# The first tiles of a two-layer hybrid-attention kernel: norm gain by VectorE shuffle, more idle products, another order of the first loads, and mixing products over 128 rows

## The chip, the cores and the metric

The kernel runs on one NeuronCore of a Trainium2 chip, in one launch. The metric is the time of an execution on the device in microseconds (us); of the kernel before there are three runs, and their median counts. Engines are named as the profile names them: PE is TensorE's products, PEld its weight loads, DVE is VectorE, ACT is ScalarE, POOL is GpSimd, SP is the queue engine that issues most DMAs.

## What is computed

Two layers over 512 tokens of 1024 features, then a last normalisation. Cut to what matters here:

```python
def rmsnorm(x, g):
    y = x * lax.rsqrt(jnp.mean(x * x, axis=-1, keepdims=True) + RMS_EPS)
    return y * g

def hybrid_layer(x, norm_g, w_in, ...):
    h = rmsnorm(x, norm_g)
    proj = h @ w_in                      # 1024 x 8388: queries, keys, values, gates
    ya = moba_attention(...);  yb = dsa_attention(...);  yc = dilated_mixture(...)
    merged = sum of sigmoid gates times (ya, yb, yc) @ w_br
    return x + merged @ w_out

def dilated_mixture(q, k, v):            # three groups with windows of their own
    ...
    w = softmax(stack(lses), axis=0)     # one weight a token, head and group
    return sum(w[..., None] * stack(outs), axis=0)
```

## The kernel before

A plan is built first: `add` records each operation with its engine, an estimate of its time, its buffers and a priority (`pri`, lower goes first), and `schedule` places them in order of start and priority on a modelled clock. What is emitted is that order; each engine runs its row of instructions in order and waits at semaphores. Priorities around -1e5 to -9e5 are those of the start.

All large products are taken in three parts, since a 32-bit number is split into a rounded upper part (`whi`, `h_hi`: a cast, L331, mostly on ACT) and the remainder (`wlo`, `h_lo`: a subtraction, L337 on POOL or L338 and L390 on DVE): hi by hi, hi by lo, lo by hi. So one tile of weights costs a DMA (`ws`), a cast, a subtraction and three products of 512 columns (L449 to L451 where the tokens are stationary, L430 to L432 where the weights are).

**The start.** x comes in four tiles t of 128 tokens, each in two halves b of 512 features (`load_x`, L286 to L296): one DMA of 256 KB for each. All go to SP's queue but the second half of tile 0, which goes to ACT's. `XPRI` sets how the later tiles stand among the first weight loads. For each tile: squares of both halves summed into `sq` (L668 ACT, L669 DVE), then `rstd`: mean plus epsilon (L738), root (L739, ACT), reciprocal (L740) and one Newton step (L741, L742, which leaves a factor -2). `norm_tile` multiplies x by that and by the gain, L711, into `h`; four transposes on PE (L717) put `h` into PSUM, a cast and a subtraction make `h_hi` and `h_lo` in the layout that the products want.

The gain `norm_g` of layer 0 is spread to 128 partitions by `first_g`: 4 KB come into one partition (`grow`, L304, third on ACT's queue), and two products of one row (L700) with a row of -0.5 (`half`) write it to PSUM as `gp`. The -0.5 undoes the factor -2. In layer 1 and for the last normalisation a DMA spreads the gain and ACT multiplies it by -0.5 (L685).

PE has idle products on zeros (`idle`, L325, `WARM` = 10 of them; `keep_warm`, L692, four after the gain and four behind each half of the transposes of tile 0) ahead of the first real one.

The first real products are `values` of the dilated groups (`c_values`): 512 columns of `w_in`, eight tiles of weights k, four tiles of tokens t. `VRUNS` lists the runs (t, first k, last k): tiles 0 and 1 take k 0 to 2 each, then 3 to 4, then 5 to 7; after that tiles 2 and 3 take all eight.

**The mixing** (`c_mix`, L1084 to L1094, once a layer): the softmax weights of the three groups are transposed into `rw`, whose other rows POOL clears first; for each pair of heads and each group one product with the constant `sel` (L1094) spreads twelve rows of `rw` over 128 partitions of `bc`, which multiplies the group's output (L1064, DVE). `rw` and `sel` are used in their rows 0 to 63. These products stand between other ones on PE in runs of 2, 1, 2 and 1.

## Time and profile before

| | |
|---|---|
| median of three runs | 1074.54 us (1073.83 to 1074.83) |
| the profiled execution, its own time | 1073.64 us |
| span of its instructions | 1071.9 us |
| PE busy | 1062.5 us (99%), 5390 products |
| PEld busy | 885.9 us (83%) |
| POOL busy | 637.5 us (59%) |
| ACT busy | 592.0 us (55%) |
| DVE busy | 510.9 us (48%) |

The execution's own time is 1.7 us longer than the span, and 0.9 us shorter than the median. Products overlap in the pipeline, so a product's duration is longer than the distance from one start to the next; distances between starts are what to read. Idle products count as busy like any others. The clock row of the page stands at full speed from the first slice on, though the first idle products are twice as far apart as the later ones; the level in the first microseconds is read from those distances.

### The profile page before, as it was taken

To read this page: it belongs to the slowest core of one execution; us is meant where nothing else is said; L and a number is where in the kernel's file an instruction comes from. 1 tells how busy PE (TensorE), PEld (TensorE's weight loads), DVE (VectorE), ACT (ScalarE), POOL (GpSimd) and SP (SyncE) were. 2 spreads that over 40 slices of the span, in tenths; PEclk is the share of its full clock that TensorE was granted. 3 is DMA by queue.
4 is the path that set the end of the run, shared out by engine and by line. 5 is a ranking of instruction groups with operands and counts; after the bars stand their busy time and mean duration, and the time that the engine had idled before them with its cause. 6 is when DMAs were issued, how large, how long until landed. Compare 5 with 4: busy or idle time off the path is not lost.

```text
span 1071.9 us, 16877 instructions
## 1 busy us (share of the span) xinstructions
PE 1062.5 (99%) x5390; PEld 885.9 (83%) x5390; DVE 510.9 (48%) x1434; ACT 592.0 (55%) x1493; POOL 637.5 (59%) x636
## 2 busy tenths in 40 slices
PE   9999999999999999999999999999999999999997
PEld 5898888888887878888888889888888878788885
DVE  5138987566642441113432589856655425311143
ACT  6444356787776653334553444568877767333441
POOL 4765754557753349776666177545666425686853
PEclk9999999999999999999999999999999999999999
DMA  7653543433431323453754155334444223336322
GB/s 227 186 125 79 148 109 83 140 83 94 120 94 51 81 60 99 110 175 98 217 160 130 30 136 145 85 95 112 112 101 119 65 52 81 87 89 194 109 81 78
DMA packets 123690, 119.00 MB, mean 111 GB/s; under 512 B 19385, under 2 KB 102225, under 8 KB 123602
## 3 DMA queue, kind: packets, MB, share of 16 engines
q1 hardware_dynamic: 123312, 117.61, 40.3%
q8 instruction: 42, 0.69, 0.3%
q14 instruction: 46, 0.38, 0.1%
q10 hardware_dynamic: 290, 0.33, 0.1%
HBM read 96.07 MB, written 6.36 MB: 96 GB/s over the span
## 4 chain that ended last, share of the span: by engine, by line
PE 98%; ACT 1%; issue 1%; DVE 0%; POOL 0%; POOLq 0%
PE pp L430 22%; PE pp L432 21%; PE pp L431 21%; PE sc L542 4%; PE pp L451 3%; PE pp L450 3%; PE pp L449 3%; PE po L1150 3%; PE po L1149 3%; PE po L1151 3%; PE tp L614 2%; PE pv L637 2%; PE pv L649 1%; PE sc L999 1%; PE pv L1037 1%; PE tpn L717 1%
## 5 line engine op out<-in xcount | busy, mean ns | idle before, releaser
L337 POOL TENSOR_TENSOR wlo<-ws,whi 128x256 fp32r<-128x256 f32 (+2 forms) x439 | 439.4, 1016 | 314.7 <-ACT whi L331 260.9
L430 PE MATMUL pp<-h_hi,whi 128*128 128x512 f32 (+1 forms) x896 | 357.1, 399 | 0.4 <-DVE gate L526 0.3
L432 PE MATMUL pp<-h_hi,wlo 128*128 128x512 f32 (+1 forms) x896 | 348.4, 389 | 0.0
L431 PE MATMUL pp<-h_lo,whi 128*128 128x512 f32 (+1 forms) x896 | 348.2, 389 | 0.0
L331 ACT CAST whi<-ws 128x256 fp32r<-128x256 f32 (+2 forms) x434 | 214.7, 508 | 236.1 <-PE pp L431 123.8
L432 PEld LDWEIGHTS pp<-h_hi,wlo 128*128 128x128 f32 x896 | 168.2, 188 | 35.1
L430 PEld LDWEIGHTS pp<-h_hi,whi 128*128 128x128 f32 x896 | 168.5, 188 | 34.3 <-issue 3.5
L431 PEld LDWEIGHTS pp<-h_lo,whi 128*128 128x128 f32 x896 | 168.6, 188 | 28.7
L873 DVE SCALAR_TENSOR_TENSOR th<-th,pp 128x512 f32<-128x512 f32 x32 | 22.0, 687 | 132.0 <-PE pp L432 126.8
L390 DVE TENSOR_TENSOR ptl<-tp,pth 128x256 fp32r<-128x256 f32 (+3 forms) x128 | 58.1, 462 | 44.0 <-ACT pth L331 43.3
L449 PE MATMUL pp<-whi,h_hi 128*128 128x512 f32 (+2 forms) x192 | 67.5, 352 | 0.0
L451 PE MATMUL pp<-whi,h_lo 128*128 128x512 f32 (+2 forms) x192 | 66.8, 348 | 0.0
L450 PE MATMUL pp<-wlo,h_hi 128*128 128x512 f32 (+2 forms) x192 | 66.7, 347 | 0.0
L331 ACT CAST pth<-tp 128x256 fp32r<-128x256 f32 (+3 forms) x128 | 50.7, 406 | 26.1 <-PE tp L614 15.0
L858 ACT ACTIVATE th<-pp 128x512 f32<-128x512 f32 x48 | 28.6, 595 | 54.6 <-PE pp L432 54.6
L552 ACT ACTIVATE p<-p,st 128x128 f32<-128x128 f32 (+3 forms) x96 | 53.5, 558 | 1.8 <-DVE st L550 1.5
L609 ACT ACTIVATE p<-p,st 128x128 f32<-128x128 f32 (+3 forms) x96 | 50.9, 558 | 1.8 <-DVE st L608 1.4
L820 DVE MATCH_REPLACE8 work<-m,work 128x512 f32<-128x512 f32 (+2 forms) x96 | 51.8, 542 | 0.1
L819 DVE MAX8 m<-work 128x8 f32<-128x512 f32 (+2 forms) x96 | 50.8, 550 | 0.7 <-POOL work L812 0.4
L430 PE MATMUL pp<-yh,whi 128*128 128x512 f32 x128 | 50.7, 396 | 0.0
L1149 PE MATMUL po<-whi,mhh 128*128 128x512 f32 x128 | 50.2, 392 | 0.0
L432 PE MATMUL pp<-yh,wlo 128*128 128x512 f32 x128 | 50.0, 391 | 0.0
(189 smaller groups left out, 1732.3 us busy)
## 6 DMA issues: line engine op xcount, KB each, us to landing
ws<-in_w_in_dram SPq DMA_DIRECT2D x192, 256.0 KB, 2.9
ws<-in_w_in_dram SPq DMA_DIRECT2D x96, 128.0 KB, 2.3
ws<-in_w_out_dram SPq DMA_DIRECT2D x32, 256.0 KB, 2.6
ws<-in_w_in_dram SPq DMA_DIRECT2D x24, 192.0 KB, 2.9
x<-x SPq DMA_DIRECT2D x16, 256.0 KB, 3.9
x<-in_x_dram SPq DMA_DIRECT2D x15, 256.0 KB, 5.1
zq<-rt SPq DMA_DIRECT2D x48, 64.0 KB, 2.8
zq<-rt SPq DMA_DIRECT2D x20, 128.0 KB, 2.4
```

The costliest lines, as they stand in the source:

```text
L331: add("act", n_act(n), lambda: nc.scalar.copy(dst(), src()), r=r, w=w, pri=pri, name=name, alt=("dve", n_dve(n, two), lambda: nc.vector.te ...
L337: add("pool", n_pool(n), lambda: nc.gpsimd.tensor_tensor(dst(), a(), b(), op), r=r, w=w, pri=pri, name=name, alt=("dve", n_dve(n), lambda: ...
L390: add("dve", n_dve(n), lambda: nc.vector.tensor_tensor(lo_fn(), src_fn(), hi_fn().bitcast(F32), ALU.subtract), r=[src, hi] if hi is not lo ...
L430: nc.tensor.matmul(o, lhs(hi.t, k % 2), a, start=(k == 0), stop=False)
L431: nc.tensor.matmul(o, lhs(hi.t, k % 2), b, start=False, stop=False)
L432: nc.tensor.matmul(o, lhs(lo.t, k % 2), a, start=False, stop=(k == nk - 1))
L449: nc.tensor.matmul(ps.t[:, :width], tokfn(h_hi, k), hi.t[:, kk, :width], start=(k == 0), stop=False)
L450: nc.tensor.matmul(ps.t[:, :width], tokfn(h_hi, k), lo.t[:, kk, :width], start=False, stop=False)
L451: nc.tensor.matmul(ps.t[:, :width], tokfn(h_lo, k), hi.t[:, kk, :width], start=False, stop=(k == KD - 1))
L552: add("act", n_act(N, True) + 190, lambda: nc.scalar.activation(p.t[:, :N], p.t[:, :N], AF.Exp, bias=nm_fn(), scale=-1.0, accum_out=s_fn() ...
L820: add("dve", n_dve(N) + 80, lambda i=i, N=N: nc.vector.match_replace(works[i].t[:, :N], m8[i].t, works[i].t[:, :N], GONE), r=[works[i], m8 ...
L1149: nc.tensor.matmul(ps.t[:, :n], mh.t[:, c], hi.t[:, kk, :n], start=(k == 0), stop=False)
```

## The change

- `first_g`, its two one-row products, `half` and the four idle products behind them go. `grow` becomes two tiles of 128x512, cleared by DVE; each half of `norm_g` comes by one small DMA into partitions 0, 32, 64 and 96 (ACT's queue, behind `ident`), and a VectorE shuffle (`spread_g`) copies the first row of each group of 32 partitions to all 32. The shuffle of the second half stands behind the first half's L711.
- Both halves of tile 0 of x go to SP's queue, first and second; `XPRI` places the other tiles anew. The preload of the root's table waits until the gain's DMAs are issued, and the first casts of the weights (`go`) wait for the first root.
- 18 idle products at the start; three and two behind the transposes of tile 0 (before: four and four).
- The constants of the root take over the factor: the mean is scaled by -4/D and the root taken with scale -1. The ACT multiplication by -0.5 becomes a plain copy in layer 1 and goes for the last normalisation.
- `VRUNS`: tiles 0 and 1 take k 0 to 4, then 5 to 7. `EARLY` goes to 0, so the first remainder is not given to DVE.
- The mixing products use all 128 rows of `rw` and `sel`; POOL clears 128 rows.

```diff
-WARM = 10
-VRUNS = ((0, 0, 3), (1, 0, 3), (0, 3, 5), (1, 3, 5), (0, 5, 8), (1, 5, 8), (2, 0, 8), (3, 0, 8))
-EARLY = 0.6
-XPRI = (0, 0.3, 1.6, 4.3)
+WARM = 18
+VRUNS = ((0, 0, 5), (1, 0, 5), (0, 5, 8), (1, 5, 8), (2, 0, 8), (3, 0, 8))
+EARLY = 0.0
+XPRI = (0, 0.6, 2.8, 4.4)
...
-        if l == 0 and t == 0 and b == 1 and not after:
-            add("act", 60, fn(nc.scalar), w=[xb], pri=-9e5, lag=2600.0)
-        else:
-            add("sp", 950 if l == 0 else 700, fn(nc.sync), r=[x1tok[t][b]] if l else (), w=[xb],
-                pri=-1e5 + XPRI[t] if t else -3e5, lag=2000.0, after=after)
+        add("sp", 950 if l == 0 else 700, fn(nc.sync), r=[x1tok[t][b]] if l else (), w=[xb],
+            pri=-1e5 + XPRI[t] if t else -3e5, lag=2000.0, after=after)
...
-            add("act", 60, lambda: nc.scalar.dma_start(grow.t[0:1, :], norm_g[0:1, :]), w=[grow], pri=-8e5, lag=3000.0)
-            add("act", 60, lambda: nc.scalar.dma_start(ident.t, k_ident), w=[ident], pri=-7e5, lag=3200.0)
+
+            add("act", 60, lambda: nc.scalar.dma_start(ident.t, k_ident), w=[ident], pri=-9e5, lag=3600.0)
+            for b in range(2):
+                add("dve", 550, lambda b=b: nc.vector.memset(grow[b].t, 0.0), w=[grow[b]], pri=-9e5)
+                loaded = add("act", 60, lambda b=b: nc.scalar.dma_start(grow[b].t[0:P:32, :], norm_g[0:1, b * T:(b + 1) * T].to_broadcast([4, T])),
+                    r=[grow[b]], w=[grow[b]], pri=-8e5, lag=2600.0)
...
-            copy(tot, lambda hi=hi: f(hi), lambda s=s: f(s), [s], [hi], pri, "whi", True)
+            copy(tot, lambda hi=hi: f(hi), lambda s=s: f(s), [s, go], [hi], pri, "whi", True)
...
-    def first_g():
...
-            add("pe", 870, lambda b=b: nc.tensor.matmul(g[b].t, half.t[0:1, 0:P], grow.t[0:1, b * T:(b + 1) * T], start=True, stop=True),
-                r=[half, grow], w=[g[b]], pri=-4e5, name="gb")
-        keep_warm(4, plan.ops[-1:])
-        return g
+    def spread_g(b, g, after):
+
+        add("dve", n_dve(T), lambda: nc.vector.stream_shuffle(g.t, grow[b].t, [0] * 32), r=[grow[b]], w=[g],
+            pri=-2e5 - 1, after=after, name="gb")
...
+            if not port and t == 0:
+                spread_g(b, gb[b], [hn] if b else ())
...
-                keep_warm(4, plan.ops[-1:])
+                keep_warm(3 - b, plan.ops[-1:])
...
-        tiny(lambda: stt(r.t[:, 1:2], c(6), -3.0, r.t[:, 0:1], op0=ALU.add, op1=ALU.mult), [st.tok], r)
+        tiny(lambda: stt(r.t[:, 1:2], c(6), 3.0, r.t[:, 0:1], op0=ALU.add, op1=ALU.mult), [st.tok], r)
...
-    preload((), -4e5)
+    preload([loaded], -4e5)
...
-            add("pool", n_pool(T) / 2, lambda: nc.gpsimd.memset(rw.t[0:64].bitcast(F32), 0.0), w=[rw], pri=pri, after=plan.ops[-1:])
+            add("pool", n_pool(T) / 2, lambda: nc.gpsimd.memset(rw.t.bitcast(F32), 0.0), w=[rw], pri=pri, after=plan.ops[-1:])
...
-                        nc.tensor.matmul(bc.t, sel.t[0:64, 2 * g + pr, :], rw.t[0:64], start=True, stop=True)
+                        nc.tensor.matmul(bc.t, sel.t[:, 2 * g + pr, :], rw.t, start=True, stop=True)
```

How the emitted rows move, engine by engine. DVE, from the first sum of squares on, before; `x_112` is the first half of tile 0 and `sq_93` holds the sums, `gp` is the spread gain and `wlo_169` the remainder of the first weight tile:

```order
L669 ISA sq_93 128x1
L738 ISA sq_93<-sq_93,invd 128x4
L738 ISA sq_93 128x1
L740 RECIPROCAL rstd_148<-sq_93 128x1
L741 SCALAR_TENSOR_TENSOR sq_93<-sq_93,rstd_148 128x1
L742 SCALAR_TENSOR_TENSOR rstd_148<-sq_93,rstd_148 128x1
L711 SCALAR_TENSOR_TENSOR h_164<-x_112,rstd_148,gp_134 128x512
L738 ISA sq_93<-sq_93,invd 128x4
L738 ISA sq_93 128x1
L338 TENSOR_TENSOR wlo_169<-ws_127,whi_162 128x512
```

and DVE after; `x_107` is the first half of tile 0, and the two `grow` tiles are the halves of the gain:

```order
L700 STREAM_SHUFFLE gp_126<-grow_91 128x512
L670 ISA junk_133,sq_109<-x_107 128x512
L670 ISA sq_109 128x1
L738 ISA sq_109<-sq_109,invd 128x4
L738 ISA sq_109 128x1
L740 RECIPROCAL rstd_154<-sq_109 128x1
L741 SCALAR_TENSOR_TENSOR sq_109<-sq_109,rstd_154 128x1
L742 SCALAR_TENSOR_TENSOR rstd_154<-sq_109,rstd_154 128x1
L711 SCALAR_TENSOR_TENSOR h_162<-x_107,rstd_154,gp_126 128x512
L700 STREAM_SHUFFLE gp_168<-grow_101 128x512
```

The two shuffles stand ahead of the square and ahead of the second half's L711, and the remainder `wlo` has left DVE.

ACT from its first row, before; `x_91` is the second half of tile 0, `x_118` the first half of tile 1:

```order
L305 DMA ident<-in_ident_dram 128x128
L293 DMA x_91<-in_x_dram 128x512
L304 DMA grow_95<-in_norm_g_dram 1x1024
L727 ACT_TABLE_LOAD
L727 ACTIVATE pre_107<-invd 128x1
L668 ACTIVATE junk_131,sq_93<-x_91 128x512
L668 ACTIVATE junk_139,sq_93<-x_118 128x512
L739 ACTIVATE sq_93<-sq_93 128x1
```

and after, where `x_118` is the second half of tile 0, `x_129` the first half of tile 1, `ws_122` the first weight tile:

```order
L302 DMA ident<-in_ident_dram 128x128
L305 DMA grow_91<-in_norm_g_dram 4x512
L305 DMA grow_101<-in_norm_g_dram 4x512
L727 ACT_TABLE_LOAD
L727 ACTIVATE pre_115<-invd 128x1
L669 ACTIVATE junk_140,sq_109<-x_118 128x512
L739 ACTIVATE sq_109<-sq_109 128x1
L332 CAST whi_150<-ws_122 128x512
L669 ACTIVATE junk_158,sq_109<-x_129 128x512
```

The root L739 of tile 0 has moved ahead of the squares of tile 1, x has left ACT's queue, and the gain takes two DMAs.

SP from its first row, before: `x_112` is tile 0, `x_118` and `x_122` tile 1, `x_158` and `x_167` tile 2:

```order
L293 DMA x_112<-in_x_dram 128x512
L293 DMA x_118<-in_x_dram 128x512
L293 DMA x_122<-in_x_dram 128x512
L284 DMA ws_127<-in_w_in_dram 128x512
L284 DMA ws_136<-in_w_in_dram 128x512
L284 DMA ws_144<-in_w_in_dram 128x512
L293 DMA x_158<-in_x_dram 128x512
L293 DMA x_167<-in_x_dram 128x512
L284 DMA ws_186<-in_w_in_dram 128x512
```

and after: `x_107` and `x_118` are tile 0, `x_129` and `x_137` tile 1, `x_175` is tile 2:

```order
L293 DMA x_107<-in_x_dram 128x512
L293 DMA x_118<-in_x_dram 128x512
L284 DMA ws_122<-in_w_in_dram 128x512
L293 DMA x_129<-in_x_dram 128x512
L293 DMA x_137<-in_x_dram 128x512
L284 DMA ws_146<-in_w_in_dram 128x512
L284 DMA ws_152<-in_w_in_dram 128x512
L284 DMA ws_164<-in_w_in_dram 128x512
L293 DMA x_175<-in_x_dram 128x512
L284 DMA ws_190<-in_w_in_dram 128x512
```

Tile 0 is whole ahead of the first weights, and tile 2 has moved behind the fourth weight tile. From the end of the products of tiles 0 and 1 on, PE's rows are the same before and after, but for the names' numbers.

## Rows read from the trace of the kernel before

**Rows 1.** Page, part 1: busy us, share of the span and instructions of each engine.
```profile
PE 1062.5 (99%) x5390; PEld 885.9 (83%) x5390; DVE 510.9 (48%) x1434; ACT 592.0 (55%) x1493; POOL 637.5 (59%) x636
```

**Rows 2.** Waits of PE, whole span: engine, line, releaser: us in total, times, longest.
```profile
PE sc L542 <- DVE mixt L550: 0.4, 2, 0.2
```

**Rows 3.** Timeline of PE from 0 to 16 us: start, us, operation [idle before].
```profile
1.00 4.45 PE L325 MATMUL warm<-idle 128*128 128x512 bf16 x10 [1.00 <-POOL idle L322]
5.38 3.78 PE L700 MATMUL gp<-grow,half 1*128 1x512 f32 x4
9.09 1.89 PE L692 MATMUL warm<-idle 128*128 128x512 bf16 x4
10.77 1.09 PE L717 MATMUL tpn<-ident,h 128*128 128x128 f32 x4
11.66 1.91 PE L692 MATMUL warm<-idle 128*128 128x512 bf16 x4
...
13.95 1.03 PE L692 MATMUL warm<-idle 128*128 128x512 bf16 x4
14.69 0.52 PE L449 MATMUL pp<-whi,h_hi 128*128 128x512 f32 x1
```

**Rows 4.** Timeline, DVE and ACT, 4 to 10.7 us.
```profile
4.01 0.69 DVE L669 CUSTOM_DVE_ANT_0 junk<-x 128x512 f32<-128x512 f32 x1 [3.09 <-DMA x<-in_x_dram]
...
6.54 0.63 ACT L668 ACTIVATE junk<-x 128x512 f32<-128x512 f32 x1 [2.79 <-DMA x<-in_x_dram]
...
7.37 0.17 DVE L738 CUSTOM_DVE_ANT_0 sq<-sq,invd 128x4 f32<-128x4 f32 x1 [2.60 <-ACT junk L668]
...
8.30 0.16 ACT L739 ACTIVATE sq<-sq 128x1 f32<-128x1 f32 x1
...
9.21 0.17 DVE L740 RECIPROCAL rstd<-sq 128x1 f32<-128x1 f32 x1 [1.66 <-ACT junk L668]
...
9.94 0.75 DVE L711 SCALAR_TENSOR_TENSOR h<-x,rstd,gp 128x512 f32<-128x512 f32 x1
```

**Rows 5.** Timeline, ACT and DVE, the same chain near the end.
```profile
1050.20 0.16 ACT L739 ACTIVATE sq<-sq 128x1 f32<-128x1 f32 x1 [5.17 <-DVE sq L738]
...
1050.38 0.17 DVE L740 RECIPROCAL rstd<-sq 128x1 f32<-128x1 f32 x1 [0.28 <-ACT sq L739]
```

**Rows 6.** Timeline, DMA issues on SP and ACT, and landing times of all x transfers until 30 us.
```profile
0.75 1.33 SPq L293 DMA_DIRECT2D x<-in_x_dram  x3
...
1.67 0.54 ACTq L304 DMA_DIRECT2D grow<-in_norm_g_dram  x1
...
DMA to landing us min/median/max: 4.2/4.7/5.1
```

**Rows 7.** Timeline of POOL, first long run of weight remainders.
```profile
17.35 5.06 POOL L337 TENSOR_TENSOR wlo<-ws,whi 128x512 fp32r<-128x512 f32 x4 [3.00 <-ACT whi L331]
```

**Rows 8.** Timeline of PE, mixing products of layer 0.
```profile
392.60 0.39 PE L431 MATMUL pp<-h_lo,whi 128*128 128x512 f32 x1
392.83 0.40 PE L432 MATMUL pp<-h_hi,wlo 128*128 128x512 f32 x1
393.16 0.73 PE L1094 MATMUL bc<-rw,sel 64*128 64x512 f32 x2
...
394.15 0.40 PE L431 MATMUL pp<-h_lo,whi 128*128 128x512 f32 x1
...
395.08 0.39 PE L432 MATMUL pp<-h_hi,wlo 128*128 128x512 f32 x1
395.40 0.50 PE L1094 MATMUL bc<-rw,sel 64*128 64x512 f32 x1
...
396.16 0.39 PE L431 MATMUL pp<-h_lo,whi 128*128 128x512 f32 x1
```

**Rows 9.** Timeline of PE's weight loads there, and all products of bc by tile.
```profile
393.16 0.29 PEld L1094 LDWEIGHTS bc<-rw,sel 64*128 64x128 f32 x2 [0.36 <-issue]
...
L1094 PE MATMUL bc<-rw,sel x12: 387/497/502, 393.2 to 925.1; 64*128 64x512 f32 x12
```

More of the change, by code (lines that the diff above doesn't have):

```diff
@@ L286, in hybrid_kernel @@
     fills = []
-    grow, half = buf("pt", [P, D], F32, "grow"), buf("rt", [P, T], F32, "half")
+    grow = [buf("rt", [P, T], F32, "grow") for _ in range(2)]
     def load_x(l, t, b, after):
@@ L316, in hybrid_kernel @@
     add("pool", 100, lambda: nc.gpsimd.memset(scol.t[64:128], 1.0), w=[scol])
-    add("pool", 100, lambda: nc.gpsimd.memset(invd.t, 1.0 / D), w=[invd])
+    add("pool", 100, lambda: nc.gpsimd.memset(invd.t, -4.0 / D), w=[invd])
     add("pool", 100, lambda: nc.gpsimd.memset(big.t, BIG), w=[big])
@@ L323, in hybrid_kernel @@
     warm = buf("pp", [P, T], F32, "warm")
-    for _ in range(WARM):
-        add("pe", 427, lambda: nc.tensor.matmul(warm.t, idle.t, idle.t[:, 0:1].to_broadcast([P, T]), start=True, stop=True), r=[idle], w=[warm], pri=-5e5, name="warm")
+    for n in range(WARM):
+        add("pe", 427 if n < 8 else 217, lambda: nc.tensor.matmul(warm.t, idle.t, idle.t[:, 0:1].to_broadcast([P, T]), start=True, stop=True), r=[idle], w=[warm], pri=-5e5, name="warm")
     bias_act = BIAS[0]
@@ L682, in load_g @@
             dma(lambda b=b: g[b].t, lambda b=b: src[:, b * T:(b + 1) * T].to_broadcast([P, T]), g[b], 725, pri=-2e5, after=fills[-30:-29])
-        o = [buf("sc", [P, T], F32, "gp") for _ in range(2)] if to_psum else g
+        if not to_psum:
+            return g
+        o = [buf("sc", [P, T], F32, "gp") for _ in range(2)]
         for b in range(2):
-            add("act", n_act(T), lambda b=b: nc.scalar.activation(o[b].t, g[b].t, AF.Copy, scale=-0.5), r=[g[b]], w=[o[b]], pri=-2e5, name="gb")
+            add("act", n_act(T), lambda b=b: nc.scalar.copy(o[b].t, g[b].t), r=[g[b]], w=[o[b]], pri=-2e5, name="gb")
         return o
@@ L693, in keep_warm @@
                 pri=-3.5e5, after=after, name="warm")
-    def first_g():
-        add("pool", 100, lambda: nc.gpsimd.memset(half.t[0:1, 0:P], -0.5), w=[half], pri=-5e5)
-        g = [buf("sc", [P, T], F32, "gp") for _ in range(2)]
-        for b in range(2):
-            add("pe", 870, lambda b=b: nc.tensor.matmul(g[b].t, half.t[0:1, 0:P], grow.t[0:1, b * T:(b + 1) * T], start=True, stop=True),
-                r=[half, grow], w=[g[b]], pri=-4e5, name="gb")
-        keep_warm(4, plan.ops[-1:])
-        return g
+    def spread_g(b, g, after):
+        add("dve", n_dve(T), lambda: nc.vector.stream_shuffle(g.t, grow[b].t, [0] * 32), r=[grow[b]], w=[g],
+            pri=-2e5 - 1, after=after, name="gb")
     def norm_tile(t, gb, pri, port=True):
@@ L726, in preload @@
         b = buf("st", [P, 8], F32, "pre")
-        add("act", 1300, lambda: nc.scalar.activation(b.t[:, 0:1], invd.t[:, 0:1], AF.Sqrt), r=[invd], w=[b], pri=pri, after=after, name="preload")
+        add("act", 1300, lambda: nc.scalar.activation(b.t[:, 0:1], invd.t[:, 0:1], AF.Sqrt, scale=-1.0), r=[invd], w=[b], pri=pri, after=after, name="preload")
     def rstd(st, pri):
@@ L737, in tiny @@
             add("dve", 120, fn, r=[st.buf, *reads], w=[st.tok if w is None else w], pri=pri, name="tiny")
-        tiny(lambda: nc.vector.tensor_tensor_reduce(st.t[:, 0:4], st.t[:, 0:4], invd.t, 1.0, EPS, ALU.mult, ALU.add, c(4)), [invd])
-        add("act", 250, lambda: nc.scalar.activation(c(5), c(4), AF.Sqrt), r=[st.buf], w=[st.tok], pri=pri, name="sqrt")
+        tiny(lambda: nc.vector.tensor_tensor_reduce(st.t[:, 0:4], st.t[:, 0:4], invd.t, 1.0, -4.0 * EPS, ALU.mult, ALU.add, c(4)), [invd])
+        add("act", 250, lambda: nc.scalar.activation(c(5), c(4), AF.Sqrt, scale=-1.0), r=[st.buf], w=[st.tok, go] if not go.writers else [st.tok], pri=pri, name="sqrt")
         tiny(lambda: nc.vector.reciprocal(r.t[:, 0:1], c(5)), [st.tok], r)
         tiny(lambda: stt(c(6), c(4), r.t[:, 0:1], r.t[:, 0:1], op0=ALU.mult, op1=ALU.mult), [r])
-        tiny(lambda: stt(r.t[:, 1:2], c(6), -3.0, r.t[:, 0:1], op0=ALU.add, op1=ALU.mult), [st.tok], r)
+        tiny(lambda: stt(r.t[:, 1:2], c(6), 3.0, r.t[:, 0:1], op0=ALU.add, op1=ALU.mult), [st.tok], r)
         return r
     tanhs, gfin = [], []
-    preload((), -4e5)
+    preload([loaded], -4e5)
     def layer(l):
-        gb = load_g(norm_g[l:l + 1, :], True) if l else first_g()
+        gb = load_g(norm_g[l:l + 1, :], True) if l else [buf("sc", [P, T], F32, "gp") for _ in range(2)]
         for t in range(4):
```

4 lines of the change are left out of this document (2 added, 2 removed).

## The prediction

> **What bounds the kernel now.** I read the page's busy times first: PE 1062.5 us of a 1071.9 us span, no other engine over 60% [rows 1]. Next PE's own list of waits: after the 1.00 us ahead of its first product [rows 3] its longest entry is 0.4 us in two places [rows 2]. PE is the bound from end to end, and two things alone can shorten the run: PE's rows that do no work for the result, and distances between starts that are longer than the columns need. Then the timeline of PE at the start [rows 3]: the first real product starts at 14.69 us. Everything ahead of it is idle products, two spread products of the gain (3.78 us) and transposes of tile 0. The last view is PE's distances around the mixing products [rows 8] with the weight loads [rows 9].
>
> The level of the clock is told by the idle products, all of one form [rows 3]: ten in 4.45 us, four in 1.89, four in 1.91, but four in 1.03 us from 13.95 on. So until about 13.5 us PE ran at 1.2 GHz, then at 2.4. Ten unbroken ones from 1.00 on did not raise it; the stretch from 9.09 on, unbroken too, had raised it some 4.4 us later. Between them stood the one-row products.
>
> **The start, step by step.** Its path is x, squares, root, L711, transposes, casts, products, and PE only follows it. All times below are in us of the span.
>
> (a) *x.* Before, the first half of tile 0 was there at 4.01 and the second, on ACT's queue, at 6.54 [rows 4]. Now the second half stands second on SP, issued near 1.2. In that place a transfer took at least 4.2 us [rows 6], which is 5.4; it had ACT's transfer beside it, which is gone, so 5.4 is the upper end. The lower is the first half's 4.0. I take 5.0, nearer the row of its own place.
>
> (b) *The gain.* DVE clears two tiles, each at most a 512-wide operation of 0.69 [rows 4], so the first DMA is issued near 1.5. Before, 4 KB issued at 1.67 [rows 6] had come by 5.38, when the product that needs it began [rows 3]: at most 3.7 us; the first half of x took 3.3. I take 3.0 for 4 KB with less ahead of it, so 4.5, with 4.0 and 5.2 as ends. The shuffle has no row; the nearest are DVE's 512-wide operations of 0.69 and 0.75 [rows 4]. I take 0.69; twice that is the upper end, and nothing below half. The Trainium skill, VectorE: DVE Perf Modes, section "The perf-mode tier table", gives a shuffle about 2400 ns for 2048 elements, an estimate of 0.6 us for 512, which would make the sum 0.2 us better; no run here shows it.
>
> (c) *Sum of squares.* DVE does the shuffle 4.5 to 5.2, then the first half's square, which had been ready since 4.0: 0.69 and a read-out, to 6.0. ACT squares the second half 5.0 to 5.9. So L738 comes near 6.05, against 7.37 [rows 4]: 1.3 us.
>
> (d) *Root.* Before, ACT squared half of tile 1 first and began the root at 8.30, 0.93 after L738; and the reciprocal came at 9.21 behind yet another square [rows 4]. Now the root is next on ACT. Near the end of the trace, with nothing between, the reciprocal starts 0.18 after the root [rows 5]; L738 to root I take as 0.28. The reciprocal is then at 6.5 instead of 9.21. From it to L711 0.73, from L711 to the transposes 0.83 [rows 3, 4]: these start at 8.1 instead of 10.77.
>
> (e) *Is PE free by then?* 18 idle products at 0.43 are 7.7 us, to 8.7, if the clock never rises; if it rises once they have run longer than the ten that did not do it, ten at 0.43 and eight at 0.23 end at 7.1. So PE is just about free; between, say 7.8. The one-row products and the four behind them hid under the chain of (d) and cost nothing by themselves. With the chain shorter they would not have been hidden.
>
> (f) *To the first product.* L711 ends at 8.0, the second shuffle and the second L711 take 0.69 and 0.75: second transposes at 9.45. They were at about 13.5 before, behind four idle products at the low clock (1.91). With 0.44 of transposes and two idle products at 0.23 the first real product comes at 10.3. ACT has by then cast one weight tile, made two squares, cast another and is at the first half's cast, five pieces of 0.6 to 0.7 after the root at 6.3: it ends near 9.8, in time. So 10.3 against 14.69: 4.4 us.
>
> (g) *What is late next.* Before, PE never waited after 14.69. Now it takes five weight tiles in a row for tile 0, which is 15 products at 0.23, 3.4 us, with two sets of transposes between, while all remainders lie on POOL at 5.06/4 = 1.27 each [rows 7]. The first is done near 8.4, then one each 1.27 from about 9.1, held up by ACT's casts: the fifth near 14.3. PE would want it at 14.2. The transposes of tile 1 wait for its root and L711 on DVE, behind the first `h_lo`: some 0.4. I charge 0.8 for these waits. From the second pass on (tile 1, same weights) the remainders are ahead. Net gain of the start: 4.4 - 0.8 = 3.6 us. Ends: 1.0 with the gain at 5.2, shuffles of 1.4 and twice the waits; 4.6 with none.
>
> **Mixing products.** Two 128-row products of 512 columns start 0.23 apart (392.60, 392.83). From 392.83 to the second product behind a pair of bc it is 1.32 us (394.15) for four distances, 0.92 expected: 0.40 lost. Around a single bc, 395.08 to 396.16, 1.08 for three distances, 0.69 expected: 0.39 lost [rows 8]. The load of bc's weights begins only with its product, where PEld was idle for 0.36, instead of under the product before [rows 9], and the next 128-row load comes late in the same way. The 12 products [rows 9] stand in runs of 2, 1, 2, 1 a layer: eight runs at 0.40 = 3.2 us. All lies on the path, since PE has no slack there. With 128 rows the form is that of its neighbours, whose loads are hidden; I take all 3.2 back. Ends: 0 and 3.3. POOL's clearing of 128 rows has the same columns per row and comes well ahead, so nothing; the two ACT multiplications of the last gain lie off the path, and the new constants of the root change no count.
>
> The Trainium skill speaks against this part: TensorE: Matmul & The Clock Gate, section "LDWEIGHTS (loading the stationary operand)", says that a load's time depends on columns, not rows, and "Why this matters for your kernels" that a single product of few rows takes as long as one of 128. By it the sum would lack these 3.2 us. The trace agrees on the load itself (0.29 for a pair of them, overlapped), not on its place.
>
> **Sum.** 1073.64 (the profiled execution) - 3.6 - 3.2 = 1066.8. The median of the runs is 0.9 above that execution: 1067.7.
>
> **Rivals.**
>
> *R1, rows are not what holds the load back.* If the load of bc waits because of its operands or of the semaphore it hangs on (one of the single ones is put down to DVE), 128 rows keep the 0.33 distances. Against it: the product behind bc, with other operands and no such wait, comes late too. Time: 1067.7 + 3.2 = 1070.9. By the page's rule above the same comes out.
>
> *R2, PE's clock falls again or rises late.* The idle products may run out near 7 us and PE then stands still until 8.1, with short bursts up to 10.3. If the first products run at 1.2 GHz for 4.4 us, as long as the trace needed, ten products at 0.43 instead of 0.23 lose 2.0, and the tail of this some tenths more; gain of the start 1.3. Time: 1070.0. For it: the first ten did not raise the clock. Against it: the one-row products, which stood between, are gone, and the breaks are about 1 us.
>
> *R3, the lead of the start is lost again.* PE is 3.6 us early, but another engine later on is not, for instance DVE with its rounds of maxima, so an old wait of 0.4 [rows 2] grows. Against it: these engines are fed by PE's own products and move with it. Time: 1067.7 + 3.6 = 1071.3.
>
> *R4, slower: the gain comes late.* On DVE the shuffle stands ahead of the first square, so everything behind it waits for a 4 KB DMA that is issued only after a memset and sits behind `ident`; SP's fourth weight tile also waits for that DMA's semaphore. Each us that it lands after 4.5 costs a us. The gain of 6.8 is used up when it lands at 11.3 us, and the run is slower by over 0.2% from 13.5 on; at 14.0 the time is 1067.7 + 9.5 = 1077.2. Against it: before, it was there by 5.4 from a later issue.
>
> **How the numbers follow.** Forecast 0.65, R1 0.12, R2 0.11, R3 0.05, R4 0.03; two of R1 to R3 at once 0.04, near 1073. The forecast's own range, from the ends of (g) and the upper one of the mixing, is 1074.5 less 7.9 to 1074.5 less 4.2: 1066.6 to 1070.3. The range for 8 in 10 reaches up to R2 and R1, and down by most of the spread of the three runs before (1.0): 1065.8 to 1071.0. A change of 0.2%, 2.1 us, is about what a measurement of this kernel can tell from none; faster than that, under 1072.4, are the forecast, R1, R2, R3: 0.92; within it 0.05; slower 0.03.
>
> **What would show it.** In the profile after: no L700 products on PE; the second half of tile 0 squared near 5.0; L738 near 6.05 and the root directly behind it; the first transposes near 8.1 and the first real product near 10.3, PE's distances of 0.23 from the first one on (not 0.43); waits of PE of at most about 0.8 between 10 and 25 us; bc rows of 128 with starts 0.23 apart. I am wrong if bc's distances stay at 0.33, if the first real product comes after 12, or if it comes near 10 and PE then waits for more than 2 us in all before 25.

## The result and the profile after

The changed kernel takes 1067.99 us in the median of six runs (1067.10 to 1069.11), the kernel before 1074.44 beside it (six runs, 1073.36 to 1075.43): a ratio of 0.9942, 95% interval 0.9931 to 0.9952. The profiled execution took 1067.53 us, with a span of 1065.7, so the span is 6.2 us shorter. The prediction was 1067.7.

The page's busy line of the changed kernel (engine, busy us, share, instructions), the counterpart of [rows 1]:

```profile
PE 1054.9 (99%) x5387; PEld 885.1 (83%) x5387; DVE 512.8 (48%) x1439; ACT 591.3 (55%) x1491; POOL 639.1 (60%) x636
```

PE is still the bound from end to end, so what was gained must lie in the two places that the prediction names. First the start. PE's timeline (start, us, operation, idle before), to be laid beside [rows 3]:

```profile
0.99 6.84 PE L326 MATMUL warm<-idle 128*128 128x512 bf16 x18 [0.99 <-POOL scol L316]
8.98 0.66 PE L717 MATMUL tpn<-ident,h 128*128 128x128 f32 x4 [1.14 <-DVE h L711]
...
10.37 0.66 PE L717 MATMUL tpn<-ident,h 128*128 128x128 f32 x4
...
11.11 0.58 PE L450 MATMUL pp<-whi,h_hi 128*128 128x512 f32 x1
11.53 0.40 PE L451 MATMUL pp<-wlo,h_hi 128*128 128x512 f32 x1
...
18.95 0.63 PE L717 MATMUL tpn<-ident,h 128*128 128x128 f32 x4 [0.22 <-DVE h L711]
```

The one-row products are gone. The transposes start at 8.98 instead of 10.77 and the first real product at 11.11 instead of 14.69: 3.58 us earlier. From the second on, products that stand next to each other start 0.22 to 0.24 apart, the distance at 2.4 GHz; the granted clock from 10 to 16 us is 1.00. DVE and ACT ahead of it, beside [rows 4]:

```profile
4.88 0.01 DVE L700 LOAD_MASK_SELECT gp<-grow  x1 [2.84 <-DMA grow<-in_norm_g_dram]
4.90 0.69 DVE L700 STREAM_SHUFFLE gp<-grow 128x512 f32<-128x512 f32 x1
5.51 0.68 DVE L670 CUSTOM_DVE_ANT_0 junk<-x 128x512 f32<-128x512 f32 x1
...
7.12 0.17 DVE L738 CUSTOM_DVE_ANT_0 sq<-sq,invd 128x4 f32<-128x4 f32 x1 [0.86 <-ACT junk L669]
...
7.52 0.17 DVE L740 RECIPROCAL rstd<-sq 128x1 f32<-128x1 f32 x1 [0.22 <-ACT sq L739]
```

```profile
6.29 0.63 ACT L669 ACTIVATE junk<-x 128x512 f32<-128x512 f32 x1 [1.69 <-DVE sq L670]
...
7.33 0.16 ACT L739 ACTIVATE sq<-sq 128x1 f32<-128x1 f32 x1 [0.35 <-DVE sq L738]
```

The gain lands at 4.88, the shuffle takes 0.69, and DVE's square follows. The row to stop at is ACT's: its square of the second half waits 1.69 us, and not for x but for DVE's square. The two squares run one behind the other, and L738 comes at 7.12, 2.24 us behind the gain.

Then the mixing products, beside [rows 8] and [rows 9]: PE's timeline, one of its weight loads, and all products of `bc` by tile (ns min/median/max, first and last start).

```profile
389.87 0.39 PE L433 MATMUL pp<-h_hi,wlo 128*128 128x512 f32 x1
390.10 0.63 PE L1094 MATMUL bc<-rw,sel 128*128 128x512 f32 x2
...
390.80 0.40 PE L432 MATMUL pp<-h_lo,whi 128*128 128x512 f32 x1
...
391.73 0.39 PE L433 MATMUL pp<-h_hi,wlo 128*128 128x512 f32 x1
391.96 0.40 PE L1094 MATMUL bc<-rw,sel 128*128 128x512 f32 x1
...
392.43 0.40 PE L432 MATMUL pp<-h_lo,whi 128*128 128x512 f32 x1
```

```profile
391.73 0.19 PEld L1094 LDWEIGHTS bc<-rw,sel 128*128 128x128 f32 x1
```

```profile
L1094 PE MATMUL bc<-rw,sel x12: 390/396/399, 390.1 to 919.3; 128*128 128x512 f32 x12
```

Around a pair it is now 0.93 us for four distances (389.87 to 390.80; before 1.32), around a single one 0.70 for three (391.73 to 392.43; before 1.08). The load stands under the product ahead, at 391.73. Eight runs at 0.38 to 0.39 are 3.1 us.

The two gains can be separated by the place of these products. The first `bc` was at 393.16 and is at 390.10: 3.06 us, of which 0.10 is its own shorter distance, so the start has given 2.96 by then. The last was at 925.1 and is at 919.3: 5.8 us. The span is 6.2 shorter. Product by product, the changed kernel is ahead by 2.95 us at 30 us (the same product starts at 33.11 before and at 30.16 after), by 2.96 ahead of the first mixing, by 4.50 behind it, by 4.58 ahead of the second and by 6.12 behind that. So the start is worth 3.0 us and the mixing 1.54 in each layer, 3.1 in all. Of the 3.58 us by which the first real product came earlier, 0.63 were lost again, all of it before 30 us.

### The profile page after: what moved, and what is told of

It reads as the page before. It is cut to its first block, busy times and chain, and to the rows that moved or that the text cites. A ratio compares the mean times of both kernels' runs of the same rounds, so it can differ in the third digit from the quotient of the medians.

```text
span 1065.7 us, 16870 instructions
## 1 busy us (share of the span) xinstructions
PE 1054.9 (99%) x5387; PEld 885.1 (83%) x5387; DVE 512.8 (48%) x1439; ACT 591.3 (55%) x1491; POOL 639.1 (60%) x636
## 4 chain that ended last, share of the span: by engine, by line
PE 96%; ACT 1%; issue 1%; DVE 1%; DMA 1%; POOL 0%; POOLq 0%; SPq 0%; DVEq 0%; ACTq 0%
PE pp L431 22%; PE pp L432 22%; PE pp L433 22%; PE sc L543 4%; PE pp L452 3%; PE pp L451 3%; PE pp L450 3%; PE po L1150 3%; PE po L1149 3%; PE po L1151 3%; PE tp L615 2%; PE pv L638 2%; PE pv L650 1%; PE sc L999 1%; PE pv L1037 1%
```

## The experiments

All times are medians of runs; the kernel before was run beside each (1073.81 to 1074.52 us in the medians). The changed kernel itself is "after".

| kernel | us, median (range, runs) | ratio to before, 95% interval |
|---|---|---|
| after | 1067.99 (1067.10-1069.11, 6) | 0.9942, 0.9931-0.9952 |
| before + mixing on 128 rows | 1071.39 (1069.64-1072.31, 8) | 0.9970, 0.9959-0.9980 |
| after, mixing on 64 rows | 1070.93 (1070.37-1071.61, 6) | 0.9968, 0.9957-0.9980 |
| after, mixing on 96 rows | 1069.90 (1 run) | |
| after, unaltered, again | 1068.42 (1067.53-1069.61, 5) | 0.9945, 0.9932-0.9957 |
| after, DVE's first square first | 1066.88 (1066.57-1067.04, 5) | 0.9930, 0.9918-0.9942 |
| the same, again | 1067.75 (1067.29-1067.90, 5) | 0.9941, 0.9927-0.9955 |
| after, ACT's sum in its own tile | 1066.96 (1066.84-1067.08, 4) | 0.9935, 0.9918-0.9951 |
| both of these | 1067.27 (1067.02-1067.44, 4) | 0.9937, 0.9923-0.9952 |
| after, x second half on ACT's queue | 1070.15 (1069.88-1070.41, 4) | 0.9960, 0.9946-0.9974 |
| after, 10 idle products | 1069.59 (1068.83-1070.82, 4) | 0.9955, 0.9939-0.9970 |
| after, 26 idle products | 1068.19 (1067.43-1068.76, 5) | 0.9945, 0.9932-0.9957 |
| before + root ahead of squares | 1074.00 (1072.97-1074.82, 10) | 0.9996, 0.9987-1.0005 |

### The two parts apart: rows of the mixing products (rival R1)

The kernel before with this alone:

```diff
-memset(rw.t[0:64].bitcast(F32), 0.0)
+memset(rw.t.bitcast(F32), 0.0)
-nc.tensor.matmul(bc.t, sel.t[0:64, 2 * g + pr, :], rw.t[0:64], ...)
+nc.tensor.matmul(bc.t, sel.t[:, 2 * g + pr, :], rw.t, ...)
```

> The kernel before with one part of the change alone: the mixing products take all 128 rows. Theory (the 64-row weight loads are not placed under the product before them, and this is all that the part is worth): starts around the bc products 0.23 us apart instead of 0.33, eight runs of 0.40 us gone, 3.1 to 3.2 us less than before, about 1071.3 us; the start of the trace unchanged, first real product near 14.7. Rival (a product of few rows costs what one of 128 rows costs, and the distances in the changed kernel come from its other edits): distances stay 0.33 and the time stays at that of before, 1074.4 us.

The changed kernel with the same lines turned back:

> The changed kernel with its mixing products back on 64 rows: the start alone. Theory (both parts add up, none covers the other): bc distances 0.33 again, 3.1 us above the changed kernel, about 1071.1 us, first real product near 11.1 us as in the changed kernel. Rival (PE's lead of the start is partly lost later on, at the mixing or elsewhere): more than 1072 us although the first real product is at 11.1.

The changed kernel with 96 rows:

```diff
-nc.tensor.matmul(bc.t, sel.t[:, 2 * g + pr, :], rw.t, ...)
+nc.tensor.matmul(bc.t, sel.t[0:96, 2 * g + pr, :], rw.t[0:96], ...)
```

> The changed kernel with the mixing products on 96 rows. Theory A (a weight load is hidden only where its rows are those of the neighbouring products, all 128): starts around bc about 0.33 us apart, some 0.40 us lost in each of the eight runs as with 64 rows, some 3 us above the changed kernel. Theory B (64 rows are a special case, half of the array): 0.23 us apart as with 128 rows and the time of the changed kernel. Theory C (the loss grows with the rows that are missing): between the two, near 0.28.

The parts add up within their intervals: 0.30% and 0.32% apart, 0.58% together. With the mixing alone the start was not quite as expected in the profiled execution: the first real product came at 15.23, not near 14.7, at a granted clock of 0.50 from 9 to 15 us. Behind it the mixing gave the same 1.54 us in each layer. The start was run as a whole; of its own parts only those in the sections below were tried apart.

With 64 rows in the changed kernel, PE's timeline and weight loads:

```profile
390.18 0.73 PE L1094 MATMUL bc<-rw,sel 64*128 64x512 f32 x2
390.83 0.50 PE L431 MATMUL pp<-h_hi,whi 128*128 128x512 f32 x1
391.17 0.40 PE L432 MATMUL pp<-h_lo,whi 128*128 128x512 f32 x1
```

```profile
390.17 0.29 PEld L1094 LDWEIGHTS bc<-rw,sel 64*128 64x128 f32 x2 [0.36 <-issue]
390.83 0.19 PEld L431 LDWEIGHTS pp<-h_hi,whi 128*128 128x128 f32 x1 [0.36 <-issue]
```

With 96 rows:

```profile
392.06 0.64 PE L1094 MATMUL bc<-rw,sel 96*128 96x512 f32 x2
392.53 0.39 PE L431 MATMUL pp<-h_hi,whi 128*128 128x512 f32 x1
```

```profile
391.83 0.42 PEld L1094 LDWEIGHTS bc<-rw,sel 96*128 96x128 f32 x2
```

With 64 rows the loads stand idle for 0.36 us both when PE goes from 128 to 64 rows and when it comes back (390.17, 390.83; behind a run of one product it is 0.24 to 0.25 on the way back), and a run of two products costs what a run of one does. With 96 rows the load lies under the product ahead, and the next product starts 0.47 behind the pair's first, which is two normal distances. So it is not the number of rows as such, nor the operands or the semaphore (R1 falls): the cost is one of changing from the 128-row form to the 64-row form and back, per run and not per product. Rows of 32 were not tried. The Trainium skill has a rule that fits, on another page than the one that the prediction weighed: TensorEngine Tiling (Array Packing), section "Tiling Modes", says that "Changing tiling mode (not just tile) drains the TensorE", and lists 64 and 32 rows as modes, but not 96. The rows agree, if a plain product of 64 rows counts as such a mode, which the page does not say: a break of 0.24 to 0.36 us in the loads at each change with 64 rows, none with 96.

The time of the 96-row kernel's one run is not the mixing's: in it the gain landed at 5.66 us and the first products were slow, as in the next section. Its span, 1068.1, is near the 1067.8 of the execution shown there, which has 128 rows and the same late start.

### What varies from execution to execution (rivals R2, R4)

The changed kernel again, unaltered:

> The changed kernel once more, unaltered, so that the kernel with DVE's first two rows exchanged has a neighbour measured in the same way. Theory: the sum of squares is serial by DVE (shuffle, square) and then ACT, and waits for a transfer whose landing varies by about a us, so the median stays near 1068.0 us with a spread of about 2 us, while the exchanged rows gave 1066.9 with a spread of 0.5. Rival: the difference of 1.1 us was chance between chips, and this run comes out at 1067.0 or below.

Its profiled execution took 1069.61 us, 2.1 more than that of the first series. PE, then DVE:

```profile
0.99 5.73 PE L326 MATMUL warm<-idle 128*128 128x512 bf16 x18 [0.99 <-POOL scol L316]
9.86 0.66 PE L717 MATMUL tpn<-ident,h 128*128 128x128 f32 x4 [3.14 <-DVE h L711]
...
13.44 0.63 PE L451 MATMUL pp<-wlo,h_hi 128*128 128x512 f32 x1
13.87 0.63 PE L452 MATMUL pp<-whi,h_lo 128*128 128x512 f32 x1
```

```profile
5.75 0.01 DVE L700 LOAD_MASK_SELECT gp<-grow  x1 [3.73 <-DMA grow<-in_norm_g_dram]
...
8.00 0.17 DVE L738 CUSTOM_DVE_ANT_0 sq<-sq,invd 128x4 f32<-128x4 f32 x1 [0.86 <-ACT junk L669]
```

Two things happen here. The gain lands 0.87 later, and L738 follows it by 2.25 us, as in after: R4's mechanism, one us for one us, only small. And the eighteen idle products are over 1.1 us sooner (5.73 instead of 6.84 us, since more of them ran at 2.4 GHz) and the transposes 0.88 later, so PE stands still for 3.14 us. By 13.44 the real products start 0.43 apart, the distance at 1.2 GHz: R2. The granted clock says the same: 0.50 from 12 to 14 us. The first real product comes 1.55 us later than in after, and by 30 us the kernel is 2.0 behind: 0.9 by the gain, the rest by the clock. The 96-row run shows the same pair (a gap of 2.99 us, then 0.43). So R2 is not a rival of the forecast but happens in some executions of it; with the late gain it makes most of the changed kernel's spread, as far as the profiled executions show. That the idle time is what lets the clock fall is tried by taking idle products away and by adding some.

With ten of them:

```diff
-WARM = 18
+WARM = 10
```

> The changed kernel with 10 idle products at the start instead of 18; all else is as in the change. Theory: the chain of the start does not need PE, but PE's clock does: the idle products end at about 5.3 us, PE stands still for some 3.5 us until the first transposes at 9.0, and the transposes and the first real products run at 1.2 GHz (starts 0.43 apart) for some 4 us; about ten to fifteen products lose 0.2 us each, so the time is 2 to 3 us above the changed kernel, near 1070.5. Rival: the eight idle products do nothing, since the transposes and the products behind them raise the clock themselves: 1068.0, starts 0.22 apart from the first real product on.

```profile
0.99 3.77 PE L326 MATMUL warm<-idle 128*128 128x512 bf16 x10 [0.99 <-POOL scol L316]
9.88 1.11 PE L717 MATMUL tpn<-ident,h 128*128 128x128 f32 x4 [5.12 <-DVE h L711]
...
13.42 0.93 PE L450 MATMUL pp<-whi,h_hi 128*128 128x512 f32 x1
14.20 0.39 PE L451 MATMUL pp<-wlo,h_hi 128*128 128x512 f32 x1
```

PE stood still for 5.12 us; the transposes took 1.11 instead of 0.66, and the first real product came 3.54 behind them instead of 2.13: the low clock. It rose again with the second real product. The granted clock was 0.50 from 9 to 14 us. So the mechanism is there, but it hits the five idle products and the transposes more than the real ones, and the cost is 1.2 to 1.6 us against after's two series, not 2 to 3. How much of that the idle products are worth stays open: beside the execution of after above, whose gain came at nearly the same time (5.75, here 5.79), the first real product is 0.76 later (13.42, 12.66), but by 30 us only 0.2 are left.

With 26:

> The changed kernel with 26 idle products at the start instead of 18. Theory: part of the changed kernel's spread (1067.1 to 1069.6) is the clock, which falls in executions in which the 18 idle products run out about 3 us ahead of the first transposes; with 26 they end at 8.3 to 9.5 us, the stretch in which PE stands still is at most 1.5 us, no real product runs at 1.2 GHz, and the time is near 1067.7 with a highest run of 1068.7 at most; where the clock rises late the idle products hold the transposes back by up to 0.5 us, so the lowest run is no lower than 1067.3. Rival: the slower executions come from the late gain alone, and the median stays at 1068.4 with the highest at 1069.5.

The median did not move (1068.19 against 1068.42 and 1067.99), the highest run fell from 1069.61 to 1068.76. The theory had put them at 1067.7 and at most 1068.7, the rival at 1068.4 and 1069.5: neither is met, and five runs do not settle whether the slowest executions are gone. The profiled one shows why the median need not move: the gain came early (4.42), the transposes waited behind the idle products (8.54), the first real product's lead over after (10.66, 11.11) was gone by 21 us, and 0.8 us were lost elsewhere, where layer 1 begins:

```profile
523.70 0.66 PE L717 MATMUL tpn<-ident,h 128*128 128x128 f32 x4 [0.64 <-DVE h L711]
```

In after the same transposes begin at 522.86 without a wait. Here ACT's copy of layer 1's gain waited for its DMA until 520.41 (in after both copies run from 518.21 on), and ACT's square stood behind it. A part of the spread is thus not from the start at all.

### The place of x (step a)

```diff
+        if l == 0 and t == 0 and b == 1 and not after:
+            add("act", 60, fn(nc.scalar), w=[xb], pri=-9.5e5, lag=2600.0)
+        else:
```

> The changed kernel with the second half of tile 0 of x back as the second transfer of ACT's queue, ahead of the gain's two. Theory: x on SP's queue as such is worth nothing, since ACT's square of the second half waits for DVE's square and not for x, and L738 is at 7.1; if the half lands at 5.4 to 6.5 as before, L738 stays within 0.3 us of 7.1, and only the gain, pushed one place back on ACT's queue, can cost: up to 0.5 us. Time 1068.0 to 1068.5. Rival (the prediction's step a): the place of x is what moved the chain, the half lands 1.5 us later and the time is 1069.5.

```profile
6.64 0.01 DVE L703 LOAD_MASK_SELECT gp<-grow  x1 [4.61 <-DMA grow<-in_norm_g_dram]
...
8.89 0.17 DVE L741 CUSTOM_DVE_ANT_0 sq<-sq,invd 128x4 f32<-128x4 f32 x1 [0.86 <-ACT junk L672]
```

(L741 here is L738 of the other kernels.) The time is near the rival's number, but by the theory's mechanism, mis-sized. L738 is again 2.25 us behind the gain; what moved is the gain, from 4.88 to 6.64. The half of x landed 4.6 us behind its issue at 1.19, near 5.8, while ACT's square of it began at 8.06, behind DVE's: x was not on the path. The clock adds to the loss: PE stood still for 4.20 us, the granted clock was 0.50 from 11 to 14 us, and the first real product came at 14.23, 3.12 later than in after for a gain that was 1.76 later. So x on SP's queue pays, not by bringing x sooner but with the gain that comes sooner. That the 256 KB now ahead of the gain on its queue delay it fits, but one trace does not show how much of the 1.76 us they are: without them the gain landed anywhere from 4.42 to 5.79, and in the kernel before the 4 KB of the gain stood behind the same transfer and had come by 5.38. All four runs are above the highest of after's eleven (1069.61).

### The sum of squares (step c)

DVE's first square ahead of its first shuffle:

```diff
-            add("dve", *on_dve, ..., name="sq", port=True)
+            sq0.append(add("dve", *on_dve, ..., name="sq", port=True))
-                spread_g(b, gb[b], [hn] if b else ())
+                spread_g(b, gb[b], [hn] if b else sq0)
```

> The changed kernel with two DVE rows exchanged: the square of the first half of tile 0 ahead of the first shuffle. Theory (in the changed kernel the shuffle's wait for the gain holds DVE's square, and ACT's square of the second half waits for DVE's since both write the same tile of sums): DVE's square at 4.0 instead of 5.5, ACT's near 4.9 instead of 6.3, L738 near 5.9 instead of 7.1, first transposes near 7.8 instead of 9.0, first real product near 10.0 instead of 11.1, the run 0.6 to 1.1 us shorter than the changed kernel. Rival (the second half of x has not come by then, or ACT's square waits for something else): L738 stays between 6.8 and 7.2 and the time is that of the changed kernel, 1068.0.

```profile
4.20 0.69 DVE L670 CUSTOM_DVE_ANT_0 junk<-x 128x512 f32<-128x512 f32 x1 [2.17 <-DMA x<-in_x_dram]
...
5.82 0.17 DVE L738 CUSTOM_DVE_ANT_0 sq<-sq,invd 128x4 f32<-128x4 f32 x1 [0.27 <-ACT junk L669]
```

L738 comes 1.3 us earlier and hangs on x, no longer on the gain. Once more, on another chip:

> The changed kernel with DVE's first square ahead of its first shuffle, once more, on the same chip as the kernel with 26 idle products. Theory: 1066.9 as before, spread under 0.7 us, first transposes near 7.7 and first real product near 10.0, since L738 hangs on x and no longer on the gain. Rival: the first measurement was a fortunate chip, and the median lies within 0.3 us of the changed kernel's 1068.0 to 1068.4.

1067.75, later than the first series by 0.9 and within 0.3 us of after's 1067.99, where the rival had put it. The ratios (0.9930 and 0.9941, after's 0.9942 and 0.9945) lie within one another's intervals, so a gain in the median is not shown by these two series. What repeats is the trace and the spread: L738 at 5.50 and the first real product at 9.80, a profiled span of 1065.3 (the shortest of its five, which reach 1066.1), and runs within 0.6 us of each other in either series, where after's two have 2.0 and 2.1.

ACT's sum in a tile of its own, with DVE's order as in the change:

```diff
+            own = buf("st", [P, 8], F32, "sqb")
+            add("act", ..., lambda: nc.scalar.activation(junk.t, xb.t[:, c], AF.Square, accum_out=own.t[:, 0:1]), r=[xb], w=[junk, own], ...)
+            add("dve", 120, lambda: nc.vector.tensor_copy(st.t[:, s4:s4 + 1], own.t[:, 0:1]), r=[own, st.buf], w=[st.tok], ...)
```

> The changed kernel with ACT's sum of the second half in a tile of its own, from which DVE copies one column into the shared tile ahead of L738. Theory: ACT's square waits for DVE's square only because both write the same small tile; now it starts when x is there, at 5.0 or before, beside DVE's, and L738 follows DVE's square and the copy: near 6.4 with the gain at 4.9 (7.1 before), first transposes 0.7 us earlier; time 1067.3 to 1067.8, spread as before since the shuffle still stands ahead. Rival: ACT's square waits for x or for the table of the root, and L738 stays 2.2 us behind the gain: 1068.0 to 1068.6.

```profile
4.57 0.63 ACT L678 ACTIVATE junk<-x 128x512 f32<-128x512 f32 x1
```

```profile
5.11 0.68 DVE L670 CUSTOM_DVE_ANT_0 junk<-x 128x512 f32<-128x512 f32 x1
...
6.27 0.17 DVE L742 CUSTOM_DVE_ANT_0 sq<-sq,invd 128x4 f32<-128x4 f32 x1
```

This settles it. With another tile to write to, ACT squares the second half at 4.57, ahead of DVE's square at 5.11; it had waited for nothing but the right to write to `sq`. The plan also moves tile 3's transposes forward by three products, near 23 us, behind all that is read here. L742 (L738 elsewhere) is 1.79 us behind the gain (4.48 here), not 2.24: 0.45 less, where 0.7 was expected, since from the start of the copy (5.96) to L742 it is another 0.31. Of all versions it has the narrowest runs. Their median is 1.0 us under after's first series, but the intervals overlap (0.9918 to 0.9951, 0.9931 to 0.9952), and the profiled span is 0.5 shorter: the earlier L742 is shown, a gain of 1 us in the time is not.

Both together:

> The changed kernel with both: DVE's first square ahead of its first shuffle, and ACT's sum in a tile of its own. Theory: both squares start as soon as their half of x is there (near 4.0 and 4.6), and L738 comes at 5.5 to 5.7, at most 0.3 us ahead of the exchanged rows alone; the time is 1066.6 to 1067.6, no further than these, since the products behind then wait for weights and remainders. Rival: the two squares touch different rows of the same chain and their gains add up: 1066.2 or less.

L738's counterpart came at 5.84, no sooner than with the exchanged rows alone, and the time was 1067.27: no addition. All three versions have the same profiled span, 1065.2. Something else is late next.

### What is late next

In after, the lead of the first product shrinks at the transposes of tile 2 (18.95, first fence of PE above). ACT, then DVE ahead of them:

```profile
15.70 0.17 ACT L739 ACTIVATE sq<-sq 128x1 f32<-128x1 f32 x1
...
16.67 0.63 ACT L669 ACTIVATE junk<-x 128x512 f32<-128x512 f32 x1 [0.25 <-DMA x<-in_x_dram]
```

```profile
17.40 0.17 DVE L740 RECIPROCAL rstd<-sq 128x1 f32<-128x1 f32 x1 [0.87 <-ACT junk L669]
```

From 18.34 to 18.95 PE's starts are 0.61 apart instead of 0.23, so 0.38 of the 0.63 us lost are here. The root of tile 2 is done at 15.9, but its reciprocal waits until 17.40 for ACT's next square, that of tile 3, which writes the same tile `sq` and waits for its x. By its releaser it is the same wait as in step c, for a write to another column of the same tile, and the same as that of the reciprocal at 9.21 in [rows 4]. The three versions of step c end at the same place. PE's transposes of tile 2 in the kernels with DVE's first square first, with ACT's sum in its own tile, and with both:

```profile
18.32 0.63 PE L717 MATMUL tpn<-ident,h 128*128 128x128 f32 x4 [0.21 <-DVE h L711]
```

```profile
18.32 0.63 PE L721 MATMUL tpn<-ident,h 128*128 128x128 f32 x4 [0.40 <-DVE h L715]
```

```profile
18.36 0.63 PE L721 MATMUL tpn<-ident,h 128*128 128x128 f32 x4
```

The first real products had come at 10.00, 10.27 and 10.43, the last of them although its transposes were early (7.70), since ACT waited 0.34 us for a weight tile ahead of the cast of `h_hi`. At tile 2 all three are 0.59 to 0.63 us ahead of after, and 0.53 to 0.57 at the end. A tile of its own for each sum is the next thing to try there; that was not run, so that the shared tile is the cause at tile 2 is read from the releaser and not shown by an experiment.

### The root ahead of the squares

The kernel before, with tile 0's root placed ahead of the squares of tile 1:

```diff
+        for o in later:          # the squares of tile 1
+            root.succ.append((o, False))
...
```

This is not the root alone. The plan placed other rows anew: the first weight remainder went from DVE to POOL, and the second half's L711 came earlier, at 9.23 instead of 11.37.

> The kernel before with one part of the change alone: tile 0's root goes ahead of the squares of tile 1 on ACT. The gain still comes through one-row products on PE with four idle ones behind them. Theory: PE is the bound of the start then: with the idle and one-row products at 1.2 GHz they end at about 10.8 us whatever the chain does, so the first transposes stay near 10.7, and the time is within 0.7 us of the kernel before, 1073.8 to 1074.5. Rival: the chain alone sets it, L711 comes 1.7 us earlier and the first real product too: 1072.8.

```profile
6.00 1.98 PE L702 MATMUL gp<-grow,half 1*128 1x512 f32 x4 [0.55 <-DMA grow<-in_norm_g_dram]
...
9.26 0.95 PE L719 MATMUL tpn<-ident,h 128*128 128x128 f32 x4 [0.30 <-DVE h L713]
10.00 1.91 PE L694 MATMUL warm<-idle 128*128 128x512 bf16 x4
```

```profile
7.72 0.17 DVE L746 RECIPROCAL rstd<-sq 128x1 f32<-128x1 f32 x1 [0.94 <-ACT junk L668]
```

No difference that can be measured (0.9996, 0.9987 to 1.0005). Step d was won only in part: the root came directly behind the sum (6.81), but the reciprocal (L746 here, L740 elsewhere) again waited for an ACT square that writes the same `sq`. From the sum to the reciprocal it is 1.13 us here (6.59 to 7.72), 1.84 before, 0.40 in after. The expected reason, PE's rows that hold the transposes near 10.7, is not what the profiled execution shows: the one-row products took 1.98 instead of 3.78 us, so the transposes could come at 9.26; four idle products at the low clock (1.91 us) then stood ahead of the second set. With the mixing alone the one-row products took 1.99 us too, and there PE waited 2.07 us for L711 and the transposes began at 10.41: without the shorter chain, PE being free does not help. That the parts of the start need each other is argued from these two traces; PE's rows were not taken out alone.

## Why the prediction came out right, and where it was off

By its steps:

- **(a) x.** The second half had landed by 4.57 in the kernel with two tiles and at 4.78 in the one with both, against 5.0 taken: at most 3.6 us behind an issue near 1.2. The 4.2 of [rows 6] was not a least time: the first half of x had taken 3.3 by the prediction's own step b. Near enough, and not on the path: see the place of x.
- **(b) The gain.** 4.88 in the profiled execution against 4.5, and 4.42 to 5.79 over the executions of the changed loads; the late end lies beyond the 5.2 allowed. Each transfer moves 8 KB (4 rows of 512), not 4. The shuffle took 0.69, the value taken from DVE's rows. The estimate worked out from the Trainium skill, VectorE: DVE Perf Modes, section "The perf-mode tier table", 0.6, is 0.09 lower; the trace decides for 0.69.
- **(c) Sum of squares.** This step failed: L738 at 7.12, not 6.05. 0.38 of the 1.07 us is the gain, the rest that ACT's square did not run beside DVE's. The prediction put both squares where their inputs are ready and did not ask what they write. [rows 4] could not show it, since ACT's square (6.54) came long after DVE's (4.01).
- **(d) Root.** Right: from L738 to the transposes 1.86 us, 2.05 taken.
- **(e) Idle products.** They ended at 7.8 as taken, but only in this execution; in others as early as 6.4, because the clock rises at another moment.
- **(f) First product.** 2.13 us behind the first transposes, 2.2 taken. So it came at 11.11 for 10.3: 1.07 too late by steps b and c, of which d and f gave back 0.26. The gain is 3.58 instead of 4.4.
- **(g) Late next.** 0.63 us were lost, 0.8 charged: the size is near, the place was partly wrong. It named the remainders on POOL and tile 1; the wait that PE's list shows, 0.38 of the loss, is tile 2's, most likely through the shared `sq`.
- **Mixing.** 3.1 for 3.2. The reason given (the load's place) was the right view. The rule of the Trainium skill that spoke against it, TensorE: Matmul & The Clock Gate, section "LDWEIGHTS (loading the stationary operand)", holds for the load by itself (182 to 186 ns with 64 rows, 187 to 188 with 128), but what was drawn from it, no gain, did not come: what costs is the change between the 64-row and the 128-row form.
- **Sum.** 1066.8 for the profiled execution, 1067.53 measured: 0.7 too much gain. Step c took 0.69 too little, the gain's landing 0.38, the mixing 0.1 too much gain; d, f and g gave back 0.43. The median lies 0.46 above that execution, not 0.9. The two errors point in opposite directions, and 0.3 us is left; that is luck, and the agreement is better than the steps deserve.
- **Ends and chances.** The ends of (g) do not follow from its terms: with the gain at 5.2, both shuffles at 1.4 and twice the waits 0.7 is left, not 1.0, and without waits it is 4.4, not 4.6. The forecast's own range would be 1066.8 to 1070.6; the median lies within either. The forecast and R1 to R3 add up to 0.93, not 0.92.
- **Rivals.** R1 falls by the 128-row and 96-row runs. R2 and R4 are real mechanisms, seen together in single executions at 2 us, not as the typical course if the medians are taken for it. R3 does not appear as it was put: the lead of 2.95 us at 30 us is the same ahead of the first mixing, and after's list of PE's waits still has the old one of [rows 2] at its old size (in the kernel with 26 idle products something of its kind does appear, where layer 1 begins):

```profile
PE sc L543 <- DVE mixt L551: 0.4, 2, 0.2
```

## What to carry to other kernels

When two engines are to work side by side, look at the tile that each one writes, down to the small column of sums: a shared one puts them in a row, whatever their inputs allow, and the trace names the other engine's write as the releaser. Where matmuls of different row counts alternate, read the distances at each change of form and not at each product; here padding the rows with zeros cost nothing that the traces show and took 0.4 us off each run of such products. Where the critical path hangs on a small transfer, look at what stands ahead of it on its queue, and do not queue work behind it that does not need it: its landing varied by over a us here.

## What was not expected of the hardware

- Products of 64 rows between products of 128 cost about 0.40 us a run, for one or two of them alike; 96 rows cost nothing (0.01 us a run over the normal distances).
- A transfer of 8 KB, issued at the same time (1.43 to 1.44 us), landed between 4.42 and 5.79 us over seven profiled executions of kernels with the same first loads, while DVE's shuffle and the chain behind it repeated within 0.01 us.
- The same eighteen idle products took 5.42 to 6.84 us, so the clock's rise comes at different moments although PE does the same. After PE stood still for 1.14 us (after) and 1.70 (two tiles) the products ran at 2.4 GHz; after 2.99 and 3.14 us the first transposes still ran at 2.4, and the work behind them at 1.2 GHz for a while; after 4.20 and 5.12 us the first transposes too ran at 1.2.
